# Partial sums added by DMA, and the prompt's weight residues read back from DRAM, in a two-sequence encoder layer

## The chip, the core and the metric

The kernel runs on one core of a Trainium2 chip. The metric is the device time of one execution in microseconds (us); the time of a version is the median of its runs. The engines named below are PE (TensorE, the matrix multiplications), DVE (VectorE), ACT (ScalarE), POOL (GpSimd) and SP (SyncE, whose queue issues the DMAs of this kernel). Each engine works through its own instructions strictly in order; semaphores order them across engines.

## The reference

One encoder layer is computed for two independent sequences, a "sample" of 1024 tokens and a "prompt" of 512 tokens, with the same weights and all in float32. Per sequence, cut to what matters:

```python
h = rms_norm(x, norm_g)
z = h @ w_in                      # 2048 -> 5632 columns = 44 blocks of 128
c_val, c_glu, c_gate, q, k, v, a_gate = split(z)
conv = pointwise(silu(layer_norm(depthwise31(c_val * sigmoid(c_glu)))))   # 1024 channels
attn = banded_sink_attention(rope(q), rope(k), v, sink)                    # window of 128
y = x + concat([conv * silu(c_gate), attn * silu(a_gate)]) @ w_out
out = rms_norm(y, final_norm_g)
```

## The kernel before

**Split products.** PE multiplies in a reduced format (fp32r), so each operand is split in two: hi is x rounded by an ACT copy, lo = x - hi by a DVE subtraction (the helper `parts`, L332 and L333). A product is three matmuls, hi·hi + hi·lo + lo·hi. The weights of 8 blocks of 128 rows make one tile `hl` of 128x(2x1024), hi half and lo half, in three rotating buffers; raw weights have three buffers `raw`. A `Prep` is one such tile: `load` issues the DMA, `make` the splitting; `w_prep` runs it two tiles ahead of PE.

**Units for the sample.** The sample's `h @ w_in` is done by a Strassen-Winograd scheme, seven block products instead of eight. A `Unit` takes two column blocks (say q head 2 and its gate) and half of the 2048 rows; its four preps (`make0` to `make3`) form sums of raw weight blocks on DVE (L130, L139, L146) and split them, and its seven steps of 12 matmuls each (L179) run on three PSUM banks. After steps 1, 4, 5 and 6 one of the four outputs (token half, column block) = (0,0), (1,1), (0,1), (1,0) is complete. There are 44 units in four stages:

- stage 0: the 8 conv column pairs (`conv0` to `conv7`), first half of the rows. The outputs are partial sums: `tap_part` copies or adds them out of PSUM (ACT L213, DVE L220) into tiles `u` and `g` and stores them to `part_*` in DRAM.
- stage 1: the same pairs, second half. Four partial sums per unit have been loaded by `load_parts` (L164) when it starts; `tap_sum` adds all seven products to them on DVE (L205), and `done` uses the finished tile: for conv, the scaling and sigmoid of `gated` (L681 to L687).
- stage 2: the other 14 pairs (gates, k/v, q with its gate), second half first, partial sums again.
- stage 3: those 14 pairs, first half, with `load_parts`, `tap_sum` and `done` (`rotate` L748 to L751, `silu_of` with `scaled` L696).

**Jobs for the prompt.** The prompt then runs 44 plain `Job`s, one column block each, over all 16 row blocks (matmuls L439): two preps per job, each a load of the same `w_in` blocks (L246) and a full split.

**Fillers and order.** The 31-tap depthwise convolution is done on DVE, one multiply-add per tap (`taps`, L720, 128x1024 for the sample). It is emitted a little at a time by a lane whose credit grows as PE work is emitted (`RATES`), as are attention and the preparation of norms. A scheduler then makes one fixed order per engine from the priorities of the instructions (`high_priority(URGENT)` for preps and taps of PSUM) and its own estimates. What it decides is fixed in the program: an engine that reaches an instruction whose input is late waits, with everything behind it.

**The prompt's norm.** `rms_ahead` (prep lane) loads `x_p`, squares it on ACT (L623) and finishes with a chain of small DVE operations (L626 to L491); then `scale_ahead` calls `spread`, which multiplies on DVE (L504) and ends in two matmuls on PE (L505).

Of the kernel before, what the change touches and what calls it, by code (L numbers as in the profile page):

```python
# [47 lines left out]
SUMS = ("A11", "A12", "S2", "s1", "S3", "S4", "A22")  # L48
# [33 lines left out]
class Unit:  # L82
# [10 lines left out]
    def __init__(self, e, w, cols, k, part, done=None):  # L93
        self.e, self.k, self.part, self.done = e, k, part, done
# [25 lines left out]
    def make0(self):  # L120
        t = self.e.hl_tile()
        if self.first:
            for h in range(2):
                self.e.parts(t[:, 0, h], t[:, 1, h], self.r1[:, h])
        else:
            self.e.parts(t[:, 0], t[:, 1], self.r1)
        return t

    def make1(self):
        add = lambda o, x, y: self.e.nc.vector.tensor_tensor(o, x, y, ALU.add)  # L130
# [7 lines left out]
    def make2(self):  # L138
        self.e.nc.vector.tensor_tensor(self.r2[:, 0], self.r2[:, 0], self.r2[:, 1], ALU.add)  # L139
        t = self.e.hl_tile()  # L140
        self.e.parts(t[:, 0], t[:, 1], self.r2)
        self.r2 = None
        return t

    def make3(self):
        self.e.nc.vector.tensor_tensor(self.r1[:, 1], self.r1[:, 1], self.t[:, 1], ALU.add)  # L146
# [11 lines left out]

    def load_parts(self):

        if self.done and not self.d:
            for n in ((0, 0), (0, 1), (1, 1), (1, 0)):
                self.d[n] = self.e.E()
                self.e.nc.sync.dma_start(self.d[n], self.part[n[0]][n[1]])  # L164
# [33 lines left out]
    def tap(self, step):  # L198
        if self.done:
            self.tap_sum(step)  # L200
        else:
            self.tap_part(step)

    def tap_sum(self, step):
        add = lambda n, b: self.e.nc.vector.tensor_tensor(self.d[n], self.bank[b], self.d[n], ALU.add)  # L205
        n = ((0, 0), (0, 0), (0, 1), (1, 1), (1, 1), (0, 1), (1, 0))[step]
        add(n, (0, 1, 0, 2, 0, 2, 0)[step])
        if step in (1, 4, 5, 6):
            self.done(n[0], n[1], self.d.pop(n))

    def tap_part(self, step):
        e, nc = self.e, self.e.nc
        copy = lambda n, b: nc.scalar.activation(self.d[n], self.bank[b], AF.Copy)  # L213
        n = ((0, 0), (0, 0), (0, 1), (1, 1), (1, 1), (0, 1), (1, 0))[step]
        b = (0, 1, 0, 2, 0, 2, 0)[step]
# [16 lines left out]
class Job:  # L232


    def __init__(self, w, ks, n, rhs, evac, before=None):
# [4 lines left out]
    def preps(self, e):  # L240
        def one(k):
            st = {}

            def load():
                st["raw"] = e.raw_tile()
                e.nc.sync.dma_start(st["raw"], self.w[:, k : k + 2 * HALF, :])  # L246

            def make():
                t = e.hl_tile()
                e.parts(t[:, 0], t[:, 1], st.pop("raw"))  # L250
# [7 lines left out]
class Encoder:  # L258
# [65 lines left out]

    def store(self, dst, src):
# [17 lines left out]
    def constants(self):  # L343
# [15 lines left out]
        def rest():  # L359
            self.ident = load("ident", [P])  # L360
            self.mask = load("mask", [3 * P])

            self.w_dw = load("w_dw", [NC, TAPS])
            nc.vector.tensor_scalar(self.w_dw, self.w_dw, -1.0, None, ALU.mult)
# [44 lines left out]
    def run(self, items):  # L409
# [3 lines left out]
        for n, item in enumerate(items):  # L413
# [3 lines left out]
            if isinstance(item[0], Unit):  # L417
                ahead = items[n + 1]
                for u in item:
                    u.open()  # L420
                    u.load_parts()
                for step in range(7):
                    for u in item:
                        late = u.product(step, late)
                    if step == 4 and isinstance(ahead[0], Unit) and len(ahead) == 1:
                        ahead[0].load_parts()
# [82 lines left out]
class Sequence:  # L509


    def __init__(self, e, s):
# [21 lines left out]
        else:  # L534
            self.h_d = dram("h_d", [self.T], NC)
            self.sums_d = {(g, n): dram(f"sum_{g}_{n}", [W], HALF) for g in (0, 1) for n in ("s1", "S2", "S3", "S4")}
# [12 lines left out]
    def block_sums(self, k0, k1, x0, x1):  # L549
# [4 lines left out]
        nc.vector.scalar_tensor_tensor(s1, x0[:, W:], col(e.norm_n, k0), t, ALU.mult, ALU.add)  # L554
# [850 lines left out]
```

## Time and profile before

| | before |
|---|---|
| median of 3 runs | 2232.35 us (2229.7 to 2236.6) |
| the profiled execution, its own time | 2230.47 us |
| its span, first to last instruction | 2228.7 us |
| PE busy | 2144.1 us, 96% |
| DVE busy | 1732.5 us, 78% |
| ACT busy | 927.5 us, 42% |
| POOL busy | 0.2 us |
| mean granted TensorE clock | 0.984 |
| DMA moved | 363.82 MB by the one queue of SP |

A row of a group reads: line, engine, operation, output<-inputs, shape, count, then busy time, mean ns of one, idle time before them and what ended it. Stages 0 to 3 of the sample fill the span up to about 950 us, the prompt's jobs with the sample's attention run to about 1520 us, and the output projections fill the rest.

### The profile page before, as it was taken

The page shows a single profiled execution, that of the slowest core. Times are in us where ns is not written, and L with a number is a line of the kernel's source. Part 1 is how long each engine was busy: PE and PEld are TensorE (multiplying, and loading weights), DVE is VectorE, ACT ScalarE, POOL GpSimd, SP SyncE. Part 2 cuts the span into 40 slices and gives each one's busy share as a digit, 9 for nine tenths or more (in the row PEclk, how much of TensorE's full clock was granted, in tenths as well). Part 3 has the DMA queues.
Part 4 walks back from the last instruction along what each step waited for, and adds up shares of the span by engine and source line. Part 5 has one row for each costly group of instructions (what it writes and reads, how often), then busy time and mean ns, then how long its engine had stood idle before and what let it go on. Part 6 is the DMA issues. An engine that isn't in the chain of part 4 may idle for free.

```text
span 2228.7 us, 26104 instructions
## 1 busy us (share of the span) xinstructions
PE 2144.1 (96%) x9510; PEld 1754.4 (79%) x9510; DVE 1732.5 (78%) x2608; ACT 927.5 (42%) x1400; POOL 0.2 (0%) x4
## 2 busy tenths in 40 slices
PE   6999998899989999999999999999999999999998
PEld 4877786688867887788888888887888778888886
DVE  8648999999999999999677879977673578446343
ACT  5455324233343222433345446654562446322232
POOL 0000000000000000000000000000000000000000
PEclk8999999899999999999999999999999999999999
DMA  8866644633365545733333533337543466527342
GB/s 285 308 202 224 216 128 165 217 129 128 132 232 170 165 142 179 242 127 121 125 113 110 168 106 117 109 119 251 170 151 109 137 213 209 171 102 264 95 133 76
DMA packets 195072, 365.48 MB, mean 164 GB/s; under 512 B 17536, under 2 KB 75264, under 8 KB 194944
## 3 DMA queue, kind: packets, MB, share of 16 engines
q1 hardware_dynamic: 194944, 363.82, 49.0%
q8 instruction: 74, 1.21, 0.2%
q14 instruction: 54, 0.44, 0.1%
HBM read 276.72 MB, written 87.03 MB: 163 GB/s over the span
## 4 chain that ended last, share of the span: by engine, by line
PE 68%; DVE 17%; DMA 9%; issue 4%; ACT 3%; SPq 0%; ACTq 0%; DVEq 0%
PE a L439 18%; PE a L179 10%; PE b L439 9%; PE c L439 9%; PE c L179 5%; DVE hl L333 3%; DVE f L720 3%; PE s L830 2%; PE b L179 2%; PE a L1165 2%; PE s L1165 2%; DMA u<-q_d 2%; PE pv L862 2%; DMA raw<-w_in 1%; PE pt L867 1%
## 5 line engine op out<-in xcount | busy, mean ns | idle before, releaser
L332 ACT ACTIVATE hl<-raw 128x1024 fp32r<-128x1024 f32 (+1 forms) x367 | 369.7, 1008 | 651.7 <-PE a L439 138.4
L333 DVE TENSOR_TENSOR hl<-raw,hl 128x1024 fp32r<-128x1024 f32 (+1 forms) x367 | 424.5, 1157 | 206.6 <-ACT hl L332 200.9
L179 PE MATMUL a<-t,hl 128*128 128x512 f32 x1968 | 487.4, 399 | 29.3 <-ACT t L335 8.5
L439 PE MATMUL a<-t,hl 128*128 128x512 f32 x2112 | 506.1, 391 | 0.0
L179 PEld LDWEIGHTS a<-t,hl 128*128 128x128 f32 x1968 | 376.7, 193 | 119.8 <-ACT t L335 8.9
L439 PEld LDWEIGHTS a<-t,hl 128*128 128x128 f32 x2112 | 393.3, 188 | 79.1
L720 DVE SCALAR_TENSOR_TENSOR f<-f,c_w_dw,f 128x1024 f32<-128x1024 f32 (+1 forms) x464 | 452.7, 1010 | 2.5 <-ACT f L715 2.4
L439 PE MATMUL b<-t,hl 128*128 128x512 f32 x1056 | 255.8, 393 | 4.4 <-ACT hl L332 2.5
L179 PE MATMUL c<-t,hl 128*128 128x512 f32 x984 | 243.8, 393 | 12.5 <-ACT t L332 7.7
L439 PE MATMUL c<-t,hl 128*128 128x512 f32 x1056 | 253.7, 392 | 0.0
L439 PEld LDWEIGHTS b<-t,hl 128*128 128x128 f32 x1056 | 196.3, 188 | 44.2 <-ACT hl L332 3.2
L179 PEld LDWEIGHTS c<-t,hl 128*128 128x128 f32 x984 | 185.7, 189 | 55.3 <-ACT t L332 9.4
L439 PEld LDWEIGHTS c<-t,hl 128*128 128x128 f32 x1056 | 197.0, 188 | 39.8
L179 PE MATMUL b<-t,hl 128*128 128x512 f32 x492 | 119.0, 389 | 0.0
L179 PEld LDWEIGHTS b<-t,hl 128*128 128x128 f32 x492 | 92.4, 188 | 19.2
L1165 PE MATMUL a<-hl,t 128*128 128x512 f32 x192 | 74.7, 390 | 0.0
L332 ACT ACTIVATE a<-pt 128x512 fp32r<-128x512 f32 x64 | 38.1, 595 | 86.4 <-PE pt L867 86.1
L830 PE MATMUL s<-t,a 128*128 128x384 f32 (+1 forms) x288 | 58.6, 329 | 9.9 <-ACT a L332 9.0
L130 DVE TENSOR_TENSOR raw<-raw,raw 128x512 f32<-128x512 f32 x82 | 56.1, 684 | 14.6 <-DMA raw<-w_in 12.3
L844 ACT ACTIVATE p<-p,tiny 128x384 f32<-128x384 f32 (+1 forms) x96 | 54.5, 570 | 29.3 <-DVE tiny L841 29.1
L333 DVE TENSOR_TENSOR a<-pt,a 128x512 fp32r<-128x512 f32 x64 | 44.0, 687 | 29.1 <-ACT a L332 28.9
L830 PEld LDWEIGHTS s<-t,a 128*128 128x128 f32 x288 | 47.8, 188 | 20.7 <-ACT a L332 13.2
(245 smaller groups left out, 2049.9 us busy)
## 6 DMA issues: line engine op xcount, KB each, us to landing
raw<-w_in SPq DMA_DIRECT2D x169, 512.0 KB, 4.0
raw<-w_out SPq DMA_DIRECT2D x64, 512.0 KB, 3.7
raw<-w_out SPq DMA_DIRECT2D x64, 256.0 KB, 3.3
raw<-w_pw SPq DMA_DIRECT2D x24, 512.0 KB, 3.6
f<-xT_s SPq DMA_DIRECT2D x38, 256.0 KB, 6.1
f<-x_s SPq DMA_DIRECT2D x16, 512.0 KB, 7.2
f<-x_p SPq DMA_DIRECT2D x13, 512.0 KB, 6.9
p<-xT_s SPq DMA_DIRECT2D x24, 256.0 KB, 3.6
```

The lines of the kernel that those rows point to most:

```text
L130: add = lambda o, x, y: self.e.nc.vector.tensor_tensor(o, x, y, ALU.add)
L179: nc.tensor.matmul(acc, hl[:, l, o, j, :], toks[j][:, r], start=step in FRESH and j == 0 and q == 0, stop=step in LAST and j == HALF - 1 a ...
L332: nc.scalar.activation(hi, x, AF.Copy)
L333: nc.vector.tensor_tensor(lo, x, hi.bitcast(F32), ALU.subtract)
L439: nc.tensor.matmul(job.acc[0], hl[:, l, kk // HALF, kk % HALF, :], r, start=i == 0 and p == 0, stop=i == nk - 1 and p == 2,)
L720: nc.vector.scalar_tensor_tensor(t, h[:, j : j + T], w(j), t, ALU.mult, ALU.add)
L830: nc.tensor.matmul(ps[:, 0:n], qs[:, x, h], k[y][:, keys], start=p == 0, stop=p == 2)
L844: nc.scalar.activation(p[:, 0:n], p[:, 0:n], AF.Exp, bias=nm[:, h : h + 1], accum_out=l[:, h : h + 1])
L862: nc.tensor.matmul(pv, v[x][:, vs], pt[:, y], start=i == 0 and p == 0, stop=i == last and p == 2)
L867: nc.tensor.transpose(tp[:, h], p[:, i * P : (i + 1) * P], e.ident)
L1165: nc.tensor.matmul(acc, self.mix[self.KS[i]][:, m, b * P : (b + 1) * P], part[l].rearrange("p a b -> p (a b)"), start=i == 0 and p == 0, s ...
```

## The change

- `make0` and `make2` also store the lo half that they made (`keep`): 512 KB and 256 KB per unit, on SP's queue. The first column block of a pair is kept whole, the second in half (`k + HALF` on), because the other half of it never appears unsummed in a unit.
- The prompt's jobs load those lo parts straight into `hl` (new lines L245 and L247, on SP): ACT still makes hi, DVE makes no lo for a first column block and half of it for a second one. The `hl` buffer is therefore taken when the load is issued, not when the split is made.
- `tap` is one function for all units: steps 0, 2, 3 and 6 copy from PSUM on ACT, steps 1, 4 and 5 add on DVE (L205 of the changed file). In a last unit the old partial sum is then added by a DMA issued on POOL that accumulates into the tile (`add_into`, new line L334); `load_parts` is gone.
- The signs of the sums go back to the plain scheme (subtractions for additions, `S1` for `s1`, no negated tap weights, values and gates). That changes no count of instructions but the one negation of `w_dw`.
- `rms_ahead` ends with `yield 15000` instead of `yield 500`: its lane pauses for 15000 ns of emitted PE work before `scale_ahead` starts.

```diff
@@ class Unit, make0
+        if self.keep:
+            self.e.store(self.keep[0][:, self.k : self.k + 2 * HALF, :], t[:, 1].bitcast(F32).rearrange("p a b c -> p (a b) c"))
@@ make1 (make2 and make3 likewise)
-        add(self.t[:, 0], self.r1[:, 0], self.r2[:, 0])
-        add(self.t[:, 1], self.t[:, 0], self.r2[:, 1])
+        self.sub(self.t[:, 0], self.r2[:, 0], self.r1[:, 0])
+        self.sub(self.t[:, 1], self.r2[:, 1], self.t[:, 0])
@@ make2
+        if self.keep:
+            self.e.store(self.keep[1][:, self.k + HALF : self.k + 2 * HALF, :], t[:, 1, 1].bitcast(F32))
@@ tap (tap_sum, tap_part and load_parts removed)
+        bank = self.bank[BANK[step]]
         if step in (0, 2, 3, 6):
             self.d[n] = e.E()
-            copy(n, b)
+            nc.scalar.activation(self.d[n], bank, AF.Copy)
         else:
-            nc.vector.tensor_tensor(self.d[n], self.bank[b], self.d[n], ALU.add)
+            nc.vector.tensor_tensor(self.d[n], bank, self.d[n], ALU.add)
         if step in (1, 4, 5, 6):
-            e.store(self.part[n[0]][n[1]], self.d.pop(n))
+            part, d = self.part[n[0]][n[1]], self.d.pop(n)
+            if self.done:
+                e.add_into(d, part)
+                self.done(n[0], n[1], d)
+            else:
+                e.store(part, d)
@@ class Job, load
+                if self.low:
+                    low, c = self.low
+                    t = st["hl"] = e.hl_tile()
+                    if c == 0:
+                        e.nc.sync.dma_start(t[:, 1].bitcast(F32).rearrange("p a b c -> p (a b) c"), low[:, i, :])
+                    else:
+                        e.nc.sync.dma_start(t[:, 1, 1].bitcast(F32), low[:, k + HALF : k + 2 * HALF, :])
@@ class Job, make
+                raw = st.pop("raw")
+                if self.low:
+                    t = st.pop("hl")
+                    e.nc.scalar.activation(t[:, 0], raw, AF.Copy)
+                    if self.low[1]:
+                        e.nc.vector.tensor_tensor(t[:, 1, 0], raw[:, 0], t[:, 0, 0].bitcast(F32), ALU.subtract)
+                    return t
@@ class Encoder
+    def add_into(self, dst, src):
+        self.nc.gpsimd.dma_start(dst, src, accum_op=ALU.add)
@@ rms_ahead
-        yield 500
+        yield 15000
...
```

What the change does to the fixed orders is shown at three places. In the rows, DMASW is the completion of a DMA issued by POOL, DMAHW of one issued by SP.

**DVE in a conv unit of stage 1**, around step 1, where output (0,0) is complete. Before, the partial sum is already in `g_351`; its scaling (L681) stands two rows behind the last addition:

```order
L205 TENSOR_TENSOR g_351_2411<-a_357_2454,g_351_2411 128x512 [waits DMAHW7_49,PE_49]
L720 SCALAR_TENSOR_TENSOR f_314_2029<-f_312_2024,c_w_dw_463,f_314_2029 128x1024
L683 TENSOR_TENSOR u_340_2279<-u_340_2279,f_244_1622 128x512 [waits Activation_49]
L205 TENSOR_TENSOR g_351_2411<-b_360_2480,g_351_2411 128x512 [waits DVE_49,PE_49]
L687 TENSOR_TENSOR g_339_2277<-g_339_2277,u_340_2279 128x512 [waits DVE_49]
L681 TENSOR_TENSOR g_351_2411<-g_351_2411,f_244_1622 128x512 [waits DVE_49]
```

In the changed kernel the scaling (now L686) of DVE's tile `g_343` waits for POOL's DMA, which can start only behind the addition L205:

```order
L205 TENSOR_TENSOR g_343_2407<-b_342_2403,g_343_2407 128x512 [waits PE_49]
L692 TENSOR_TENSOR g_334_2322<-g_334_2322,u_339_2379 128x512 [waits DMASW5_49,DVE_49]
L344 TENSOR_TENSOR hl_344_2428<-raw_327_2252,hl_344_2428 128x512 [waits DMAHW1_49,Activation_49]
L725 SCALAR_TENSOR_TENSOR f_309_2083<-f_307_2078,c_w_dw_509,f_309_2083 128x1024
L132 TENSOR_TENSOR raw_350_2499<-raw_345_2431,raw_341_2392 128x512 [waits DMAHW5_49,DMAHW2_49,DVE_49]
L686 TENSOR_TENSOR g_343_2407<-g_343_2407,f_244_1681 128x512 [waits DMASW0_49]
```

Later in the same unit, on the same engine, outputs (0,1) (`u_347`) and (1,0) (`u_353`) follow:

```order
L205 TENSOR_TENSOR u_347_2447<-c_346_2443,u_347_2447 128x512 [waits PE_49]
L344 TENSOR_TENSOR hl_351_2502<-raw_350_2499,hl_351_2502 128x1024 [waits DMAHW4_49,Activation_49]
L725 SCALAR_TENSOR_TENSOR f_308_2082<-f_307_2078,c_w_dw_509,f_308_2082 128x1024
L725 SCALAR_TENSOR_TENSOR f_309_2083<-f_307_2078,c_w_dw_509,f_309_2083 128x1024 [waits DVE_49]
L692 TENSOR_TENSOR u_347_2447<-u_347_2447,g_343_2407 128x512 [waits DMASW2_49]
L344 TENSOR_TENSOR hl_354_2527<-raw_345_2431,hl_354_2527 128x1024 [waits PE_49,Activation_49]
L686 TENSOR_TENSOR u_353_2518<-u_353_2518,f_244_1681 128x512 [waits DMASW3_49]
```

Four rows stand between an addition and the first use of its tile at (0,0), three at (0,1). Such a unit has 25 DVE rows before, 4 of them taps of the convolution, and 23 now, 6 of them taps.

**DVE in a q unit of stage 3**, around steps 4 and 5. Before, for outputs (1,1) (`u_732`) and its neighbours, no row waits for a partial sum that was not loaded a unit earlier:

```order
L205 TENSOR_TENSOR g_731_5378<-a_738_5433,g_731_5378 128x512 [waits DMAHW2_49,DMAHW1_49,PE_49]
L750 TENSOR_TENSOR u_730_5376<-u_730_5376,f_687_4993 128x512 [waits DVE_49]
L205 TENSOR_TENSOR u_732_5380<-c_746_5500,u_732_5380 128x512 [waits PE_49]
L751 TENSOR_TENSOR u_730_5376<-u_730_5376,g_743_5478 128x512 [waits DVE_49]
L333 TENSOR_TENSOR hl_747_5518<-raw_741_5448,hl_747_5518 128x1024 [waits DMAHW7_49,Activation_49]
```

In the changed kernel, on the same engine, with `u_763` for (1,1) and `g_762` for (0,1), scaled by L701:

```order
L205 TENSOR_TENSOR u_763_5779<-a_751_5689,u_763_5779 128x512 [waits PE_49]
L132 TENSOR_TENSOR raw_760_5749<-raw_760_5749 128x512
L132 TENSOR_TENSOR raw_755_5707<-raw_755_5707,raw_765_5820 128x512 [waits DVE_49]
L205 TENSOR_TENSOR g_762_5765<-c_761_5761,g_762_5765 128x512 [waits DMAHW7_49,PE_49]
L725 SCALAR_TENSOR_TENSOR f_633_4887<-f_621_4844,c_w_dw_509,f_633_4887 128x1024
L701 TENSOR_TENSOR u_763_5779<-u_763_5779,f_244_1681 128x512 [waits DMASW1_49]
L344 TENSOR_TENSOR hl_766_5823<-raw_765_5820,hl_766_5823 128x1024 [waits DMAHW2_49,Activation_49]
L701 TENSOR_TENSOR g_762_5765<-g_762_5765,f_244_1681 128x512 [waits DMASW2_49]
```

Again four rows, three short and one tap, stand between the addition and the use at (1,1); the splitting L344 of the next weights stands behind that wait. At (0,0) there are four such rows too. A q unit has 25 DVE rows now, 4 of them taps; before it has 26 or 27 with 1 or 2 taps.

**PE where the prompt's norm is spread**, in stage 2. Before, the two matmuls of `spread` follow a full step:

```order
L179 MATMUL b_449_3224<-t1_217_1530,hl_440_3140 128x512 x3
L179 MATMUL b_449_3224<-t1_218_1533,hl_440_3140 128x512 x3
L179 MATMUL b_449_3224<-t1_219_1536,hl_440_3140 128x512 x3
L505 MATMUL s_432_3098<-u_433_3099,ones_r_192 128x512 [waits DVE_49]
L505 MATMUL s_432_3098<-u_434_3105,ones_r_192 128x512 [waits DVE_49]
L179 MATMUL a_418_3021<-t1_258_1678,hl_420_3029 128x512 [waits Activation_49]
```

In the changed kernel PE has them (L510) 45 matmuls later:

```order
L178 MATMUL a_436_3250<-t1_227_1629,hl_435_3236 128x512 x3
L178 MATMUL a_436_3250<-t1_228_1632,hl_435_3236 128x512 x3
L510 MATMUL s_444_3288<-u_445_3289,ones_r_192 128x512 [waits DVE_49]
L178 MATMUL a_436_3250<-t1_229_1635,hl_435_3236 128x512 x2
L510 MATMUL s_444_3288<-u_446_3295,ones_r_192 128x512 [waits DVE_49]
L178 MATMUL a_436_3250<-t1_229_1635,hl_435_3236 128x512
```

On PE the spread has moved from the end of one unit's step to the middle of another's, 45 matmuls on; on DVE more rows of other work stand between the norm's small operations and the multiplications (now L509) that feed it.

More of the change, by code (lines that the diff above doesn't have):

```diff
@@ L138, in make2 @@
     def make2(self):
-        self.e.nc.vector.tensor_tensor(self.r2[:, 0], self.r2[:, 0], self.r2[:, 1], ALU.add)
+        self.sub(self.r2[:, 0], self.r2[:, 1], self.r2[:, 0])
         t = self.e.hl_tile()
@@ L157, in open @@
         self.tags = tags
[L159 to L164, printed above, removed]
     def product(self, step, late):
@@ L232, with __init__ @@
 class Job:
-    def __init__(self, w, ks, n, rhs, evac, before=None):
+    def __init__(self, w, ks, n, rhs, evac, before=None, low=None):
+        self.low = low
         self.w, self.ks, self.n, self.rhs, self.evac = w, ks, n, rhs, evac
@@ L581, in first_sums @@
             sums = self.block_sums(j, j + HALF, x[j], x[j + HALF])
-            for name in ("S2", "s1", "S3", "S4"):
+            for name in ("S2", "S1", "S3", "S4"):
                 self.token_sum(name, 0, j, sums[name])
@@ L882, in units @@
         e, w = self.e, self.e.a["w_in"]
+        e.low = {}
         def both(cols, name, done):
             part = [[e.tc.dram_tile([P, W], F32, name=f"part_{name}_{t}{c}") for c in range(2)] for t in range(2)]
-            return lambda g, last: Unit(e, w, cols, 2 * HALF * g, part, done if last else None)
+            keep = [e.tc.dram_tile([P, ND, P], F32, name=f"low_{name}_{c}") for c in range(2)]
+            for c in range(2):
+                e.low[cols[c]] = (keep[c], c)
+            return lambda g, last: Unit(e, w, cols, 2 * HALF * g, part, done if last else None, keep)
         def each(first, second):
@@ L893, in units @@
         for i in range(0, NC, 2):
-            done = each(self.silu_of(self.gate_d[i], 1.0), self.silu_of(self.gate_d[i + 1], -1.0))
+            done = each(self.silu_of(self.gate_d[i]), self.silu_of(self.gate_d[i + 1]))
             gates.append(both((GATE + i, GATE + i + 1), f"gate{i}", done))
         rest = gates[:2] + [
-            both((K + g, V + g), f"kv{g}", each(self.rotate(self.k_d[g]), self.negative_value(g))) for g in range(2)
+            both((K + g, V + g), f"kv{g}", each(self.rotate(self.k_d[g]), self.value_of(g))) for g in range(2)
         ]
@@ L900, in units @@
             turn = self.rotate(self.q_d[h // GROUP][:, h % GROUP])
-            rest.append(both((Q + h, AG + h), f"q{h}", each(turn, self.silu_of(self.ag_d[h], -1.0))))
+            rest.append(both((Q + h, AG + h), f"q{h}", each(turn, self.silu_of(self.ag_d[h]))))
         return conv, rest + gates[2:]
```

66 lines of the change are left out of this document (25 added, 41 removed).

## The prediction

> **What bounds the kernel now.** I read the page first, then busy time by windows, then the waits, then single stretches in order of time.
>
> ```profile
> span 2228.7 us, 26104 instructions
> PE 2144.1 (96%) x9510; PEld 1754.4 (79%) x9510; DVE 1732.5 (78%) x2608; ACT 927.5 (42%) x1400; POOL 0.2 (0%) x4
> 80.00:120.00 40.00, 37.85 (x166) 30.71 (x165) 21.82 (x30) 20.18 (x33) 0.00 (x0) 1.00 0.91 303
> 240.00:360.00 120.00, 119.29 (x526) 98.12 (x525) 118.36 (x154) 37.87 (x47) 0.00 (x0) 1.00 0.43 140
> 372.00:384.00 12.00, 10.18 (x43) 7.53 (x41) 12.00 (x14) 5.52 (x9) 0.00 (x0) 1.00 0.78 269
> 384.00:420.00 36.00, 21.42 (x81) 17.10 (x81) 34.06 (x51) 9.97 (x15) 0.00 (x0) 0.76 0.51 184
> 440.00:600.00 160.00, 159.73 (x705) 131.77 (x704) 156.50 (x170) 57.51 (x74) 0.00 (x0) 1.00 0.41 138
> 700.00:920.00 220.00, 215.23 (x943) 174.06 (x942) 217.72 (x300) 61.12 (x75) 0.00 (x0) 1.00 0.51 169
> 960.00:1520.00 560.00, 556.07 (x2584) 461.57 (x2583) 462.68 (x782) 278.23 (x452) 0.00 (x0) 1.00 0.37 123
> 286.44 5.44 PE a L179 x24
> 305.49 5.44 PE a L179 x24
> ```
>
> The window rows give stretch and length, then busy time of PE, its weight loads, DVE, ACT and POOL, the granted clock, the DMA share and GB/s. PE is the bound nearly everywhere, and its work does not change: the change can only fill or open gaps on PE. But in the units DVE is as full as PE: 118.36 of 120 us in stage 1, 156.50 of 160 in stage 2, 217.72 of 220 in stage 3. The last two rows, from the chain of waits, are one step pair of two neighbouring conv units: a unit lasts 19.05 us at full pace, 84 matmuls of 5.44/24 = 0.227 us. In stage 3, 943 matmuls are 11.2 units in 220 us, 19.6 us each; there DVE is already slightly the slower one. So whatever makes DVE stand still in stages 1 and 3 reaches PE almost one for one. In the prompt (960 to 1520) PE has 556 of 560 us and DVE has room.
>
> There is one large gap, in the chain's words and in the order of time:
>
> ```profile
> PE s L505 <- DVE u L504: 16.7, 2, 14.6
> 385.20 0.16 DVE L626 TENSOR_TENSOR tiny<-sq 128x4 f32<-128x4 f32 x1 [0.63 <-ACT f L623]
> 398.67 1.58 PE L505 MATMUL s<-u,ones_r 128*128 128x512 f32 x2 [14.58 <-DVE u L504]
> ```
>
> PE stands 14.58 us for the spread of the prompt's norm, because nine small DVE operations in a row (L626 to L499) each take their turn between filler taps of about 1.2 us.
>
> **The change, part by part.** Prices on DVE come from starts in its full stretch, and the rest from groups:
>
> ```profile
> 303.57 0.68 DVE L139 TENSOR_TENSOR raw<-raw 128x512 f32<-128x512 f32 x1
> 304.17 0.68 DVE L146 TENSOR_TENSOR raw<-raw,raw 128x512 f32<-128x512 f32 x1
> 304.77 1.27 DVE L720 SCALAR_TENSOR_TENSOR f<-f,c_w_dw,f 128x1024 f32<-128x1024 f32 x1
> 305.97 0.68 DVE L205 TENSOR_TENSOR u<-c,u 128x512 f32<-128x512 f32 x1
> L205 DVE TENSOR_TENSOR u<-a,u 128x512 f32<-128x512 f32 x40 | 27.4, 684 | 0.9 <-PE a L179 0.5
> L213 ACT ACTIVATE u<-a 128x512 f32<-128x512 f32 x40 | 23.8, 594 | 59.9 <-PE a L179 52.4 <-DVE g L687 4.2 <-DMA gate_d<-u 3.3
> L333 DVE TENSOR_TENSOR hl<-raw,hl 128x1024 fp32r<-128x1024 f32 x83 | 101.2, 1219 | 36.5 <-ACT hl L332 36.2
> ```
>
> A 512-wide row costs DVE 0.60 us (303.57 to 304.17), a 1024-wide one 1.20 (304.77 to 305.97).
>
> *The pause.* With 15000 ns of emitted work between norm and spread, the small chain runs beside a step's products, and the spread stands 45 matmuls later, 10.2 us, behind work that PE has. From 372 to 420 us PE did 43 + 81 = 124 matmuls, 28.1 us worth in 48: 19.9 are lost there, the stall, 1 to 2 us before it and the half clock behind it. I take 19 back.
>
> *Prompt without lo.* 22 first column blocks x 2 preps = 44 preps lose a row of 1.22 us, 54 us; the 44 preps of second blocks lose half a row each, 44 x 0.6 = 26: together 80 us of DVE. The prompt's window has PE at 99%: worth nothing. What comes instead is 88 loads (33 MB; at 37% DMA share there is room) that wait on SP for PE to release an `hl`. Two tiles of 24 matmuls, 10.9 us, lie between release and use. Raw loads of that size land in 4.5 us (below). Queued behind a waiting one are stores and the `q_d` loads of attention, later by up to 5 us at times; bounds 0 and 6 us in all, I take 2.
>
> *Storing lo.* 88 stores on SP. Where DMA has room they cost nothing; from 80 to 120 us its share is already 0.91 and two units bring 1.5 MB more in 40 us, 39 GB/s on 303. Bounds 0 and 8 us, I take 2, since PE lost only 2 us in that window.
>
> *Adds to ACT and DMA.* In 22 last units four DVE additions each go (88 x 0.60 = 53 us), four ACT copies of 0.59 come; ACT is a third busy there, and it frees PSUM sooner. But the order gives the freed time to taps: a conv unit goes from 25 rows with 7 wide ones (3 splittings, 4 taps) to 23 with 9, and 7 x 1.20 + 18 x 0.60 = 19.2 equals 9 x 1.20 + 14 x 0.60 = 19.2 us. Measured it was 118.36/6.3 units = 18.8; over the eight units the new rows average 0.4 lighter, so about 0.6 us per unit stay free. A q unit now has 25 rows, 7 wide: 19.2 us, all full.
>
> *The new wait.* Behind the addition that completes (0,0), DVE has four other rows, 0.6 + 0.6 + 1.2 + 0.6 = 3.0 us, and then needs the accumulated tile. At (0,1) of a conv unit it has three wide rows, 3.6; at (1,1) of a q unit 3.0 again. The other outputs fall behind these waits. Let L be the time from the end of the addition to the landed sum. DVE stands (L - 3.0) + (L - 3.6) in a conv unit and 2(L - 3.0) in a q unit. Behind the waiting row stand the forming and splitting of the next weights, for which PE waits, and the step-4 addition, which PE needs before step 6.
>
> No run shows an accumulating DMA or one from POOL. The nearest rows are SP's loads in stages 1 and 3:
>
> ```profile
> raw<-w_in SPq DMA_DIRECT2D x16, 512.0 KB, 4.5
> g<-part_conv SPq DMA_DIRECT2D x12, 256.0 KB, 3.0
> u<-part_conv SPq DMA_DIRECT2D x12, 256.0 KB, 3.5
> g<-part_q SPq DMA_DIRECT2D x16, 256.0 KB, 2.9
> raw<-w_in SPq DMA_DIRECT2D x23, 512.0 KB, 4.5
> DMA to landing us min/median/max: 2.5/3.2/6.5
> ```
>
> The first three and the last row (of `part_conv`) are of stage 1, the other two of stage 3. The same 256 KB as a plain load take 3.2 us; an accumulate reads two tiles of 256 KB, as many bytes as the 512 KB load of 4.5. Bounds are 3.0 (a plain load, POOL as quick as SP) and 6.5 (the longest). I take L = 4.4, close to the row with the same bytes. Then a conv unit waits 1.4 + 0.8 = 2.2, less 0.6 free: 1.6 x 7 = 11 us (the first unit takes its sums early). A q unit becomes 19.2 + 2.8 = 22.0 against 19.6: 2.4 x 13 = 31 us (14 units, two of them run together). PE is two weight tiles ahead at the start, which swallows some 3 us once.
>
> The Trainium skill's page "DMA: Bandwidth & Descriptors" (section "Anatomy of one DMA — SWDGE (gpsimd) path") fits 2.0 us plus bytes/436e3 to a DMA from GpSimd, an estimate of 2.6 us for 256 KB; by it no wait would remain. No run here shows such a DMA, and the plain loads above are slower than that under this traffic.
>
> Sum: -19 + 2 + 2 + 11 + 31 - 3 = +24 us on the profiled execution's own 2230.5, 2254.5; that execution lies 1.9 below the median of the runs, so I say 2255.
>
> **The rivals.** *A, the waits are covered (faster).* Place: the same two rows per unit; it decides at L = 3.7, where 2(L - 3.0) x 13 and the rest make up for the pause. At L = 3.2 a conv unit loses nothing and a q unit 19.6 - (19.2 + 0.4) = 0: -19 + 4 - 3 = -18, 2212; at 3.0 another 5 less. For it: the plain loads' 3.0 and 2.9, and fewer loads on SP. Against: two streams instead of one, and a longer way to start. This is the case of the page's fit above.
>
> *B, they cancel.* At L near 3.9 (conv 1.2 - 0.6, q 1.8 - 0.4) it is 4 + 18 + 4 - 3 - 19 = +4, about 2234.
>
> *C, a longer way.* POOL's generation in software, sums issued in a cluster, 39 GB/s of stores beside them: L = 5.5 makes 3.8 x 7 + 4.6 x 13 = 86, net +68, 2298. For it stands the maximum of 6.5.
>
> That the pause does nothing (another late load of `x_p`) would add up to 19 to each.
>
> **How the numbers follow.** A measurement of this kernel can tell about 0.3%, 7 us, from no change. My forecast (L from 4.0 to 5.0, 2240 to 2278) has 0.43, A 0.33, B 0.13, C 0.11. Slower is forecast and C, 0.54; same B, 0.13; faster A, 0.33. The likeliest is 2255; the range for 8 in 10 leaves out the ends of A and half of C: 2208 to 2290.
>
> **What the profile after would show.** The L505 wait (then L510) should fall from 14.6 us to under 2, with the clock at 1.00 around 400 us. DVE should show idle time released by the DMA into tiles `g` and `u`, at L686, L692, L701 and L753, 20 to 60 us in all, and a unit period of 20 to 22 us in stage 3; POOL's issues should land 4 to 5 us after issue. In the prompt DVE should lose 80 us of splitting with PE unmoved. I am wrong if those DVE waits are under 10 us: then L was below 3.7. I am wrong in another way if they are there and PE still keeps 19.05 us a unit, because PE is then further ahead of DVE than I read.

## The result and the profile after

The changed kernel takes 2351.43 us (median, 2349.44 to 2354.78), the kernel before 2231.02 us in the same comparison: a ratio of 1.0537, interval 1.0513 to 1.0562. It is 5.4% slower, 96 us above the 2255 us of the forecast and outside its range. The ratios here and below are those on record; they can differ a little from the ratio of the two medians.

From the page of the changed kernel its span and its busy times, and then its busy time by windows (columns as in the prediction):

```profile
span 2353.0 us, 26578 instructions
PE 2186.8 (93%) x9510; PEld 1781.2 (76%) x9510; DVE 1613.1 (69%) x2475; ACT 971.7 (41%) x1488; POOL 76.9 (3%) x92
```

```profile
80.00:120.00 40.00, 39.75 (x175) 32.58 (x174) 26.18 (x36) 19.21 (x29) 0.00 (x0) 1.00 0.93 332
384.00:420.00 36.00, 32.05 (x134) 25.82 (x133) 33.80 (x44) 13.83 (x21) 0.00 (x0) 0.95 0.72 241
700.00:920.00 220.00, 180.07 (x716) 143.30 (x715) 161.92 (x209) 69.05 (x100) 29.61 (x34) 0.90 0.62 162
1100.00:1520.00 420.00, 416.38 (x1933) 346.05 (x1932) 281.42 (x543) 204.60 (x333) 0.00 (x0) 1.00 0.57 182
```

DVE has 119 us less work than before (1613.1 against 1732.5), and the kernel is longer. From 700 to 920 us DVE, once full at 217.72 of 220 us, is busy for 161.92, and PE makes 716 matmuls instead of 943: 25.8 us a unit, where it was 19.6. The granted clock there fell from 1.00 to 0.90.

The waits of DVE for the summing transfers, all eleven groups (total us, times, longest us), and PE's two largest waits:

```profile
DVE u L753 <- DMA g<-part_q: 41.2, 16, 3.7
DVE u L692 <- DMA u<-part_conv: 20.6, 7, 7.0
DVE g L701 <- DMA g<-part_gate: 18.2, 8, 4.9
DVE u L701 <- DMA u<-part_gate: 13.1, 7, 2.7
DVE g L686 <- DMA g<-part_conv: 12.7, 7, 2.2
DVE u L701 <- DMA u<-part_q: 12.3, 8, 1.8
DVE u L686 <- DMA u<-part_conv: 7.5, 5, 2.2
DVE u L753 <- DMA g<-part_kv: 5.3, 3, 2.1
DVE u L701 <- DMA u<-part_kv: 4.2, 2, 2.4
DVE g L701 <- DMA g<-part_q: 3.0, 3, 1.6
DVE g L692 <- DMA g<-part_conv: 2.6, 1, 2.6
...
PE a L178 <- DVE u L205: 40.5, 9, 7.6
PE a L178 <- DVE g L205: 23.6, 9, 5.8
```

The eleven groups sum to 141 us in 67 waits. In front of PE stands then the addition L205, which has to read a bank before PE may go on, and which is queued on DVE behind one of these waits. In the kernel before, PE's larger wait for that addition was small:

```profile
PE a L179 <- DVE g L205: 4.8, 7, 2.4
```

Where the time went, by units: the start of every 84th product of the units (line L178, or that of the same matmul in the other kernels), counted in each trace, as a lag behind the kernel before in us; negative is ahead. The first column is that start in the kernel before. A unit has 84 products; the first two units of stages 0, 1 and 3 run interleaved, as a pair. The runs named in the heads are explained below.

| before, at | place | after | low_loaded | plain_pool | later_use | pause_only | rate_no_pause | pause_rate | deep_rate2 |
|---|---|---|---|---|---|---|---|---|---|
| 207.4 | stage 1, middle of its first pair | -0.3 | -0.2 | -0.8 | -1.9 | -0.6 | -0.1 | -1.0 | +0.8 |
| 365.2 | stage 2, second unit: the unit of the stall | +38.3 | -5.1 | +18.3 | +31.8 | +0.6 | +0.2 | -1.0 | +3.4 |
| 405.1 | the next one | +17.4 | -26.0 | -2.7 | +10.9 | -20.3 | -1.6 | -21.9 | -17.5 |
| 424.2 | and the next | +18.5 | -7.7 | -1.5 | +11.4 | -9.1 | -1.6 | -14.4 | -16.9 |
| 634.3 | stage 3, first product | +18.9 | -5.6 | -0.5 | +13.4 | -9.8 | -1.6 | -14.8 | -17.5 |
| 690.7 | stage 3, third unit | +33.4 | +6.5 | +7.9 | +9.7 | -0.2 | -13.9 | -20.8 | -28.8 |
| 936.8 | last product of the units | +111.7 | +6.1 | +55.2 | +29.0 | -0.3 | -17.7 | -25.2 | -33.6 |
| 2044.4 | last product of the jobs | +124.4 | +16.3 | +68.2 | +47.8 | +3.8 | +6.5 | -5.6 | -29.5 |

The changed kernel loses 38.6 us in stage 1 (with the first unit of stage 2, into which the last sums of stage 1 reach), wins 20.9 where the stall was, keeps nearly all of that through stage 2, loses 14.5 at the change to stage 3, 78.3 in the rest of stage 3 and 12.7 in the prompt.

One q unit of stage 3 shows the loss at work. DVE's rows around the four outputs, in order of time:

```profile
844.15 0.68 DVE L205 TENSOR_TENSOR g<-b,g 128x512 f32<-128x512 f32 x1
...
849.89 0.69 DVE L753 TENSOR_TENSOR u<-g,f 64x512 f32<-64x512 f32 x1 [2.06 <-DMA g<-part_q]
...
854.26 0.69 DVE L205 TENSOR_TENSOR u<-a,u 128x512 f32<-128x512 f32 x1
...
859.52 0.69 DVE L701 TENSOR_TENSOR u<-u,f 128x512 f32<-128x512 f32 x1 [1.64 <-DMA u<-part_q]
...
862.62 0.69 DVE L701 TENSOR_TENSOR g<-g,f 128x512 f32<-128x512 f32 x1 [1.27 <-DMA g<-part_q]
...
868.06 0.69 DVE L753 TENSOR_TENSOR u<-g,f 64x512 f32<-64x512 f32 x1 [3.58 <-DMA g<-part_q]
```

and, from the same stretch, POOL's issues and the wait of PE that follows:

```profile
845.24 0.88 POOL L334 DMA_DIRECT2D g<-part_q  x1 [10.11 <-DVE g L205]
855.35 0.87 POOL L334 DMA_DIRECT2D u<-part_q  x1 [9.23 <-DVE u L205]
857.15 0.86 POOL L334 DMA_DIRECT2D g<-part_q  x1 [0.93 <-DVE g L205]
861.52 0.86 POOL L334 DMA_DIRECT2D g<-part_q  x1 [3.51 <-ACT g L203]
```

```profile
855.00 8.20 PE L178 MATMUL a<-t,hl 128*128 128x512 f32 x24 [5.49 <-DVE u L205]
```

All four outputs wait: 2.06 + 1.64 + 1.27 + 3.58 = 8.55 us in one unit. The first addition ends at 844.83, POOL starts 0.4 us later, and DVE goes on at 849.89: 5.06 us from addition to use. The fourth output, (1,0), is no addition but a copy on ACT. PE's 24 products then take 8.20 us where they need 5.44; the granted clock is 0.50 from 853.4 to 860.2 us. The Trainium skill's page "TensorE: Matmul & The Clock Gate" (section "What's actually happening") puts an idle PE back to half clock after a window of some 3.4 us; this row, behind 5.49 us of idling, agrees with it. Over all 22 units, counted by the order of POOL's issues, the waits are 22 at (0,0) with 45.3 us, 14 at (1,1) with 25.1, 14 at (0,1) with 31.4 and 17 at (1,0) with 39.0.

### The profile page after: what moved, and what is told of

Same layout as the page of the kernel before. It is cut to its first block, busy times and chain, and to the rows that moved or that the text cites. A ratio compares the mean times of both kernels' runs of the same rounds, so it can differ in the third digit from the quotient of the medians.

```text
span 2353.0 us, 26578 instructions
## 1 busy us (share of the span) xinstructions
PE 2186.8 (93%) x9510; PEld 1781.2 (76%) x9510; DVE 1613.1 (69%) x2475; ACT 971.7 (41%) x1488; POOL 76.9 (3%) x92
## 4 chain that ended last, share of the span: by engine, by line
PE 57%; issue 22%; DMA 9%; DVE 7%; POOL 3%; ACT 2%; SPq 1%; POOLq 0%; ACTq 0%; DVEq 0%
PE a L444 17%; PE c L444 9%; PE b L444 9%; PE a L178 5%; DMA u<-q_d 3%; PE c L178 2%; PE s L835 2%; DVE f L725 2%; PE a L1174 2%; PE s L1174 2%; DVE hl L344 2%; POOL g L334 2%; PE pv L867 2%; DMA raw<-w_in 1%; DMA u<-ag_d 1%
## 5 line engine op out<-in xcount | busy, mean ns | idle before, releaser
L178 PE MATMUL a<-t,hl 128*128 128x512 f32 x1968 | 514.9, 415 | 105.0 <-DVE u L205 40.5
L178 PEld LDWEIGHTS a<-t,hl 128*128 128x128 f32 x1968 | 394.7, 203 | 204.3 <-DVE u L205 44.5
L444 PE MATMUL a<-t,hl 128*128 128x512 f32 x2112 | 506.4, 392 | 0.0
L444 PEld LDWEIGHTS a<-t,hl 128*128 128x128 f32 x2112 | 394.0, 188 | 79.9
L343 ACT ACTIVATE hl<-raw 128x1024 fp32r<-128x1024 f32 (+1 forms) x279 | 275.9, 990 | 431.1 <-PE a L444 82.8
L344 DVE TENSOR_TENSOR hl<-raw,hl 128x1024 fp32r<-128x1024 f32 (+1 forms) x279 | 317.7, 1139 | 159.7 <-ACT hl L343 154.6
L178 PE MATMUL c<-t,hl 128*128 128x512 f32 x984 | 248.7, 400 | 20.1 <-DVE t L344 7.7
L178 PEld LDWEIGHTS c<-t,hl 128*128 128x128 f32 x984 | 188.9, 193 | 65.2 <-DVE t L344 11.3
L253 ACT ACTIVATE hl<-raw 128x1024 fp32r<-128x1024 f32 x88 | 93.0, 1058 | 118.3 <-PE a L444 45.3
L178 PE MATMUL b<-t,hl 128*128 128x512 f32 x492 | 119.2, 390 | 0.2
L178 PEld LDWEIGHTS b<-t,hl 128*128 128x128 f32 x492 | 92.2, 188 | 20.4 <-DVE t L347 0.8
L132 DVE TENSOR_TENSOR raw<-raw,raw 128x512 f32<-128x512 f32 x123 | 84.4, 686 | 23.9 <-DMA raw<-w_in 20.8
L344 DVE TENSOR_TENSOR a<-pt,a 128x512 fp32r<-128x512 f32 x64 | 44.1, 689 | 73.5 <-ACT a L343 73.3
L203 ACT ACTIVATE u<-a 128x512 f32<-128x512 f32 x56 | 33.4, 596 | 97.7 <-PE a L178 95.9
L835 PE MATMUL s<-t,a 128*128 128x384 f32 (+1 forms) x288 | 59.4, 335 | 14.4 <-ACT a L343 13.8
```

What stands on the lines that cost most here:

```text
L132: self.e.nc.vector.tensor_tensor(out, x, y, ALU.subtract)
L178: nc.tensor.matmul(acc, hl[:, l, o, j, :], toks[j][:, r], start=step in FRESH and j == 0 and q == 0, stop=step in LAST and j == HALF - 1 a ...
L203: nc.scalar.activation(self.d[n], bank, AF.Copy)
L253: e.nc.scalar.activation(t[:, 0], raw, AF.Copy)
L343: nc.scalar.activation(hi, x, AF.Copy)
L344: nc.vector.tensor_tensor(lo, x, hi.bitcast(F32), ALU.subtract)
```

## The experiments

Theory W: DVE's waits for the summing transfers are the loss. Theory T: the added traffic is. Theory D came after the first of these runs: DVE's amount of work sets the time of the units, and a stall of PE that is taken away only moves.

### One part at a time

pause_only is the kernel before with one line changed:

```diff
-        yield 500
+        yield 15000
```

> The kernel before with the one longer pause ahead of the prompt's spread, nothing else. In the changed kernel the unit that held the 14.6 us stall took 19.0 us where before it took 40.0, and the lag to the kernel before fell from 38.3 to 17.4 us. If the pause alone did that: 2231 - 20 = 2211 us (2208 to 2215), the spread's wait under 1 us. Rival: it was the other edits (rows of DVE saved by ACT copies and transfers) that let the norm's small operations through in time; then the pause alone gives under 8 us, 2223 to 2231.

Measured: 2238.47 us against 2237.11, ratio 1.0006 (0.9996 to 1.0015). No change: both expectations missed. PE's waits between 380 and 700 us, in the kernel before:

```profile
PE s L505 <- DVE u L504: 14.6, 1, 14.6
PE a L179 <- DVE t L336: 7.0, 2, 4.8
```

and in pause_only:

```profile
PE a L179 <- DVE t L336: 16.6, 2, 14.4
PE s L505 <- DVE u L504: 5.2, 1, 5.2
```

The two waits sum to 21.6 us before and to 21.8 us here. The stall left its place (20.9 us gained, as in the changed kernel) and came back: 11.2 us in the next unit, where the spread now stands with 5.2 us of wait, and 9.6 us between 634 and 691 us at the change of stages, where PE waits for the operand sums that DVE makes late (L336). The changed kernel has that second wait too, at the same place and 15.6 us long (the sums are L347 there); low_loaded, without the summing transfers, has 16.4:

```profile
PE a L178 <- DVE t L347: 18.3, 2, 15.6
```

low_loaded is the changed kernel with its 88 partial sums loaded a unit ahead and added on DVE, as before the change; acc_only is the changed kernel without the low parts:

```diff
low_loaded:
+    def load_parts(self): ...
-        if step in (0, 2, 3, 6):
+        if step in (0, 2, 3, 6) and not self.done:
-                e.add_into(d, part)
acc_only:
-            return lambda g, last: Unit(e, w, cols, 2 * HALF * g, part, done if last else None, keep)
+            return lambda g, last: Unit(e, w, cols, 2 * HALF * g, part, done if last else None)
-        job = lambda c, evac: Job(w[c], list(range(ND)), self.T, self.rhs, evac, low=e.low[c])
+        job = lambda c, evac: Job(w[c], list(range(ND)), self.T, self.rhs, evac)
```

> The changed kernel with the partial sums loaded a unit ahead and added on DVE again, as before the change; low parts, signs and pause stay. Theory W (DVE's waits for the summing transfers are the loss): units of stages 1 and 3 are back at 19.0 to 20 us, and the whole stands at 2211 for the pause plus up to 10 us that the prompt's jobs lost in the changed kernel: 2211 to 2224 us. Theory T (the 33 MB of low parts stored and 33 MB loaded crowd the transfers, and all that waits for DMA is late): 2260 to 2310 us, with long waits for raw weights.

> The changed kernel without the low parts (neither stored nor loaded; the prompt splits its weights itself); summing transfers, signs and pause stay. Theory W: the units lose nearly what they lost, 2351 less the 10 us of the prompt's jobs and a few us of quicker transfers, 2325 to 2345 us. Theory T: most of the loss goes, 2215 to 2260 us, and the summing transfers land in about 3 us.

low_loaded: 2246.51 us, ratio 1.0047 (1.0032 to 1.0062). acc_only: 2340.03 us, ratio 1.0460 (1.0442 to 1.0477). Without the summing transfers nearly the whole loss is gone; without the low parts nearly all of it stays. Theory T falls. (low_loaded missed its upper end of 2224 by 22.5 us, about the 20 that the pause did not give.) What T keeps is small: with the low parts' traffic the waits for summing transfers total 141 us, without it 127.

### What the wait is made of

plain_pool turns each summing transfer into a plain load over the same tile, from the same place in POOL's queue; the load overwrites what the last unit of a column pair summed, so the second half of the rows is then missing from the conv columns and the first half from the others.

```diff
-        self.nc.gpsimd.dma_start(dst, src, accum_op=ALU.add)
+        self.nc.gpsimd.dma_start(dst, src)
```

> The changed kernel with the 88 summing transfers turned into plain loads of the partial sum over the tile, issued at the same places on POOL (the first half of the rows is then missing from the sample's products). It asks what in the 4.5 us from issue to landing is the summing. If the summing is (two tiles read, one written): landing 3.0 to 3.3 us as on SP before, each of some 75 waits 1.2 us shorter, 2255 to 2275 us. If it is POOL's way of issuing: landing 4.0 to 4.6 us and 2335 to 2355 us.

Measured: 2294.79 us, ratio 1.0261 (1.0245 to 1.0276), between the two expectations. Times from issue to landing of the 88 transfers, first in the changed kernel, then in plain_pool:

```profile
DMA to landing us min/median/max: 3.8/4.7/9.1
```

```profile
DMA to landing us min/median/max: 2.8/3.5/8.1
```

The summing costs 1.1 us at the median (4.65 less 3.53 before rounding) and 1.0 at the least. DVE's waits fall from 141 to 84 us, by 57, and the time by 57 us. The expectation let some 75 waits lose 1.2 us each; 61 remain of 67, at 1.37 us on average instead of 2.10.

### The cover

calm_use takes the use of a summed tile out of the urgent rows, later_use also puts it off by six evacuations, so that more DVE rows stand between an addition and the wait:

```diff
                 e.add_into(d, part)
-                self.done(n[0], n[1], d)
+                e.held.append((e.turns + 6, self.done, (n[0], n[1], d)))
...
                         late = u.product(step, late)
+                        self.settle(self.turns)
```

`settle` calls what is due in `held`; calm_use has 0 in place of 6.

> The same with the use only taken out of the urgent rows, not put off: a median of 4.8 us of rows in between. By the order, waits behind additions of 33 us instead of 112, and those behind ACT's copies partly covered. Theory W: 2250 to 2285 us. Rival S: 2325 to 2355 us.

> The changed kernel with the use of a summed tile (scaling, rotation) put off by six evacuations and taken out of the urgent rows, so that the fixed order has a median of 8.7 us of DVE rows between an addition and the first use of its tile, where the changed kernel has 3.0 us. By the two orders and 5.0 us from addition to landed sum, the waits behind additions go from 112 to 20 us. Theory W (these waits are the loss, one for one): 2351 less 90 to 120, 2230 to 2265 us. Rival S (the loss is in the transfers' load on the memory and on POOL, or in the copies on ACT, and the waits only show it): 2325 to 2355 us. A third case: tiles held longer run short (four of each kind) and give new waits on ACT's copies; then 2270 to 2320 us with those waits in the trace.

calm_use: 2311.44 us, ratio 1.0330 (1.0288 to 1.0372), DVE's waits 63 us in 43. later_use: 2276.93 us, ratio 1.0169 (1.0134 to 1.0203), waits 44.5 us in 27. Both are better than the changed kernel by far, with the same transfers, the same copies on ACT and the same traffic: rival S falls. later_use lies in the range of its third case (tiles that run short), but hardly by that cause: ACT's copies wait 15.0 us for stores out of their tiles, 2.0 in the changed kernel, and PE waits no longer for these copies than there (17.3 us against 18.4). Both missed theory W's range on the slow side: the waits left are more than the order had let expect (63 and 44.5 us, with 33 and 20 expected behind additions), above all in stage 1, where they fell least (43 us in the changed kernel, 30 and 32 here). What is left in later_use, its largest groups:

```profile
DVE u L696 <- DMA u<-part_conv: 13.5, 7, 3.6
DVE u L702 <- DMA u<-part_conv: 12.0, 6, 4.5
```

In stage 3 its waits are 12 us instead of 97, and from 690.7 us to the end of the units it loses 19.3 us where the changed kernel lost 78.3.

### DVE's work and the pause

pause_rate is pause_only with other filler rates, rate_no_pause the same rates with the pause of before:

```diff
-RATES = (0.4, 0.9, 0.3, 1.0)
+RATES = (0.4, 0.8, 0.3, 1.05)
```

> The kernel before with the longer pause and, in stage 2, a filler rate of 0.8 instead of 0.9, with 1.05 instead of 1.0 in the prompt: some 17 taps, 20 us of DVE, leave stage 2 for the prompt. With the pause alone the 21 us gained at 365 us came back as 11 us in the next unit and 8.5 us at 634 us. Theory D (DVE is full from 225 to 950 us, and its work sets the time there, so a stall of PE taken away moves): with the taps gone the gain stays, 2237 less 8 to 20 us. Rival: the give-backs are the chain of small operations itself, whatever else DVE does: within 4 us of 2237.

> pause_rate without its pause (500 ns as before), the rates alone. Theory D (DVE's work sets the time): the stall of 14.6 us at the spread sits in front of the taken-out taps, so part of it stays, and part of pause_rate's 7 us goes: 2230 to 2237 us. Rival: the pause never mattered, 2226 to 2230 us.

pause_rate: 2229.05 us against 2236.11, ratio 0.9959 (0.9942 to 0.9977), at the upper end of theory D's range. rate_no_pause: 2235.51 us against 2237.14, ratio 0.9994 (0.9983 to 1.0004), inside it. Over the whole kernel neither the pause nor the rates are worth anything alone, and together they give 0.4%. In rate_no_pause the spread's wait is still there:

```profile
PE s L505 <- DVE u L504: 11.8, 1, 11.8
```

The table of lags shows more than the whole does. At 690.7 us the pause alone is 0.2 us ahead, the rates alone 13.9, both 20.8; at the end of the units 0.3, 17.7 and 25.2. So in the units less work on DVE brings the time by itself, most of it at the change of stages, and the pause is worth some 7 us on top of it where alone it is worth nothing. Theory D holds there. Both runs then lose most of it at the start of the prompt, in one wait of PE for the splitting of the prompt's operands, rate_no_pause first and then PE's wait at that place in the kernel before:

```profile
PE b L439 <- ACT t L335: 14.4, 1, 14.4
```

```profile
PE b L439 <- ACT hl L332: 2.5, 1, 2.5
```

In pause_rate it is 14.3 us; deep_rate (below), with rates lower still, does not have it. What makes it was not taken apart.

low_rate is low_loaded with rates 0.4, 0.75, 0.25, 1.1; deep_rate is pause_only with the same rates and no low parts; low_rate_pool is low_rate with the loads of low parts issued on POOL (`sync` becomes `gpsimd` in the two lines); low_rate2 and deep_rate2 are low_rate and deep_rate at 0.3, 0.65, 0.2, 1.2.

> The changed kernel without summing transfers (low parts and pause stay), with filler rates of 0.75 in stage 2, 0.25 in stage 3 and 1.1 in the prompt: some 25 taps in stage 2 and 8 in stage 3, 40 us of DVE, go to the prompt, where the low parts freed 80 us. Theory D: 2246 less 15 to 35 us, so 2211 to 2231 us, ahead of the kernel before if the 10 us that the prompt lost do not grow. Rival: PE's stalls in the units are not DVE's doing, 2240 to 2250 us.

> The kernel before with the longer pause and the rates of low_rate (0.75 in stage 2, 0.25 in stage 3, 1.1 in the prompt), without low parts. low_rate took 2218 us. If the rates did that and the low parts only cost: 2205 to 2216 us. If the low parts give the prompt the DVE time that the moved taps need: 2222 to 2232 us, no better than pause_rate's 2229, with PE standing in the prompt.

> low_rate with the 88 loads of low parts issued on POOL instead of SP. In the prompt low_rate lost 12 us against its own units, with SP waiting for PE to release the weight tile ahead of attention's loads. If the queue behind that wait is the loss: 8 to 12 us less than low_rate, 2206 to 2212 us. If it is the 33 MB themselves: within 3 us of low_rate's 2218. If POOL's later landing (3.5 us at the median as a plain load in the units) makes the weights late: above 2222 us.

> low_rate with lower rates still: 0.3, 0.65 and 0.2 in stages 1 to 3, 1.2 in the prompt; some 15, 17 and 9 taps more leave the units. Theory D: stage 3 and the start of the prompt lose their last DVE backlog, a further 3 to 10 us, 2208 to 2215 us; it stops paying where PE is the bound again in the units (19.05 us each). If the taps now crowd the prompt, 2218 to 2228 us.

> The kernel before with the pause and the rates of low_rate2 (0.3, 0.65, 0.2, 1.2), without low parts. At 0.75, 0.25, 1.1 the kernel without low parts was 5 us ahead of the one with them. If the low parts only cost, here too: 2192 to 2199 us against low_rate2's 2201. If the prompt needs the DVE time that they free once 40 taps more come to it: 2203 to 2215 us.

| | time, us | ratio | interval | units end, us | from there to the last job's product |
|---|---|---|---|---|---|
| kernel before | 2235.63 to 2237.14 | 1 | | 936.8 | 1107.6 |
| pause_only | 2238.47 | 1.0006 | 0.9996 to 1.0015 | 936.5 | 1111.7 |
| rate_no_pause | 2235.51 | 0.9994 | 0.9983 to 1.0004 | 919.1 | 1131.8 |
| pause_rate | 2229.05 | 0.9959 | 0.9942 to 0.9977 | 911.6 | 1127.1 |
| low_loaded | 2246.51 | 1.0047 | 1.0032 to 1.0062 | 942.9 | 1117.9 |
| deep_rate | 2213.09 | 0.9893 | 0.9879 to 0.9906 | 911.4 | 1116.0 |
| low_rate | 2218.10 | 0.9899 | 0.9854 to 0.9944 | 911.3 | 1120.6 |
| low_rate_pool | 2219.48 | 0.9929 | 0.9914 to 0.9943 | 913.0 | 1118.2 |
| deep_rate2 | 2194.64 | 0.9822 | 0.9806 to 0.9838 | 903.2 | 1111.8 |
| low_rate2 | 2201.26 | 0.9837 | 0.9820 to 0.9854 | 899.9 | 1114.8 |

The two last columns are from one profile each. low_rate, deep_rate, low_rate_pool and deep_rate2 each came out in one of their expected ranges (theory D; the low parts only cost; the transfers, not the queue; the low parts only cost); low_rate2 came out 7 us under its lowest. With the pause, taps moved from the units to the prompt are worth 1.1 and 1.8%; what these two lower rates are worth without it was not run. The low parts are worth nothing at any of the three rates: 3 to 6 us more pass in the prompt each time than without them, and the DVE time that they free is not missed. SP's queue is not the reason (low_rate_pool is no faster than low_rate); what remains is the transfers themselves, and how they cost was not taken apart. deep_rate2 beats both kernels; its window around the spread and PE's wait there:

```profile
384.00:420.00 36.00, 36.00 (x159) 29.49 (x158) 34.82 (x54) 12.46 (x17) 0.00 (x0) 1.00 0.64 222
```

```profile
PE s L505 <- DVE u L504: 2.2, 1, 2.2
```

Last, the rates of low_rate2 in the changed kernel (after_rate) and in later_use (later_rate):

> The changed kernel, summing transfers as they are, with the rates of low_rate2. Theory W: the waits stand in the fixed order whatever fills DVE; fewer taps give fewer rows between an addition and its use (by the order 148 us of waits at 5.0 us of transfer, 112 before), so of the 45 us that the rates gave the loaded version little is left: 2325 to 2350 us. Theory D alone (the loss is DVE's load, and the waits are where it shows): the rates give their 45 us here too, 2300 to 2312 us.

> later_use with the rates of low_rate2: summing transfers, uses put off, 40 taps fewer in the units. Whether the transfers can pay for the 88 additions that they save. By the order 84 us of waits at 5.0 us, 20 in later_use, against some 50 us of DVE rows fewer: 2270 to 2300 us by theory W. If DVE has so much room now that its waits no longer reach PE: 2195 to 2215 us, at or under low_rate2's 2201.

after_rate: 2336.46 us, ratio 1.0449 (1.0435 to 1.0463), DVE's waits 175 us. later_rate: 2282.76 us, ratio 1.0206 (1.0193 to 1.0220), waits 85 us. Both fall into theory W's ranges. Of the 45 us that these rates gave low_loaded (2246.5 to 2201.3), 15 are left in the changed kernel, and later_use has nothing of them, its waits having doubled: a tap taken away is a row less between an addition and its wait. Relieving DVE helps little where its queue stands at a transfer.

## Why the prediction was wrong

The direction was the forecast's likeliest, the size was not. By its own steps:

| term | forecast, us | measured, us | by |
|---|---|---|---|
| the pause | -19 | 0 | pause_only |
| prompt without lo, storing lo | +2, +2 | +8 together | low_loaded less pause_only (they differ in the signs too) |
| waits in stage 1 | +11 | +38.6 | lag from -0.3 at 207.4 us to +38.3 at 365.2; low_loaded goes by -4.9 there |
| waits in stage 3 | +31 | +78.3 | lag from 690.7 on; low_loaded goes by -0.4 there |
| PE's lead | -3 | not told apart | |

The measured terms sum to 125 us; the profiles of the two kernels lie 124 us apart and the medians 120.

**The new wait** is the step that failed most: 42 us forecast, 117 measured. The mechanism was right: same rows, DVE first, then PE through L205. Two sizes in it were wrong. The first is the count: "The other outputs fall behind these waits" let two outputs per unit wait, 44 in all; 67 of the 88 did, and in the q unit above all four. Behind the first wait DVE is late, but so is what leads to the next output: each transfer starts 0.4 us behind its own addition (855.35 behind 854.95), so it is later by as much, and little is gained for it. (1,0), for which the forecast had nothing, is the longest wait in that unit and 39 us over all, since its tile comes from a copy at the last step, with only one splitting, 1.2 us, between the wait before it and its use on DVE.

The second is L. The 4.4 us taken from the load "with the same bytes" was nearly the landing (4.7 at the median), but L runs from the end of the addition and also has POOL's start, 0.4 us: 5.06 us in the example, 4.9 at the median of the 57 additions that the trace links to an issue, and 6.4 behind 20 copies of (1,0); why these land later was not taken apart. Per q unit the forecast was 2.8 us of waits, the unit shown has 8.55, and the eight q units together have 56.5 us, 7.1 each.

The break-even of rival A at L = 3.7 fell with the count and with the pause: plain_pool has 0.4 + 3.5 = 3.9, where rival B's sum without the pause's 19 us comes to +23 us, and plain_pool is 58 us slower than the kernel before.

The Trainium skill's fit (page "DMA: Bandwidth & Descriptors", section "Anatomy of one DMA — SWDGE (gpsimd) path"), an estimate of 2.6 us for these bytes, lies below every landing here: plain transfers from POOL took 2.8 at the least and 3.5 at the median, summing ones 3.8 and 4.7. The measurement decides.

**The pause** was read off the wrong engine. "From 372 to 420 us ... 19.9 are lost there" is true of PE; the same quoted rows had DVE at 12.00 of 12 and 34.06 of 36 us in that stretch. DVE, full on both sides of PE's stall, had no time to give back. The text said that the chain "runs beside a step's products" and named no later place for its DVE rows; pause_only named it. In the changed kernel the gain stayed through stage 2 (+17.4 to +18.9), and the change to stage 3 then took 14.5 us, with PE's wait of 15.6 us for the operand sums, 4.8 before.

**The prompt** came out as forecast on DVE and worse by a few us on PE. The splitting of weights, before and after, and the half splittings that stay:

```profile
L333 DVE TENSOR_TENSOR hl<-raw,hl 128x1024 fp32r<-128x1024 f32 (+1 forms) x367 | 424.5, 1157 | 206.6 <-ACT hl L332 200.9 <-DMA f<-x_p 4.2
```

```profile
L344 DVE TENSOR_TENSOR hl<-raw,hl 128x1024 fp32r<-128x1024 f32 (+1 forms) x279 | 317.7, 1139 | 159.7 <-ACT hl L343 154.6
L255 DVE TENSOR_TENSOR hl<-raw,hl 128x512 fp32r<-128x512 f32 x44 | 30.3, 689 | 29.6 <-ACT hl L253 27.2 <-DMA hl<-low_gate 2.2
```

That is 424.5 - 317.7 - 30.3 = 76.5 us of DVE, 80 forecast, "worth nothing" as said. **Storing lo** cost nothing between 80 and 120 us (39.75 of 40 us of PE, 37.85 before). The wait of the spread (now L510) did fall, to 0.3 us, though the clock from 384 to 420 us was 0.95 and not 1.00, and the DVE waits stand at L686, L692, L701 and L753 as forecast, at 141 us instead of 20 to 60.

What stays open: how much of the loss in stage 3 is the half clock behind PE's stalls. PE's busy time for the same 9510 products is 42.7 us longer than before, but PE waits for DVE there, and no run here has the waits without the clock.

## What to carry to other kernels

A wait on an engine's queue is priced from the end of the producer to the use, the issuing engine's start included, for every output that has one; on a full engine most of it is paid (141 us of waits, 106 us in the units against low_loaded), and a saving of rows on that engine makes it longer, since the rows were its cover. Before a stall is booked as a gain, look at what the engine that is waited for does during it: if that one is full, the stall moves, and it is less work for that engine that brings the time (in the units 0.3 us by the shift alone, 17.7 by fewer taps alone, 25.2 by both). Fillers of a full engine belong to the stage that has room, and the place where they go has to be looked at too: there rate_no_pause lost again all that it had won and pause_rate most of it, while deep_rate and deep_rate2, with lower rates still, kept 1.1 and 1.8%.

## What the runs showed of the hardware

A summing DMA from POOL lands 1.1 us later at the median than a plain one of the same 256 KB from the same place (4.65 against 3.53 us), and POOL's own busy time for 88 issues and four small fills is 76.9 us against 47.6. POOL starts such an issue 0.4 us after the addition that it waits for has ended.
